# First stage of a hybrid attention block: fixed places for the row sums' transposes, the scaled keys, the query tables, the first gates' weights and the memory's norm

## The chip, the core and the metric

The kernel runs on one core of a Trainium2 chip. A core has five engines with instruction streams of their own: TensorE (PE in the profile; its weight loads are listed as PEld), VectorE (DVE), ScalarE (ACT), GpSimd (POOL) and SyncE (SP), which here issues the DMAs. Matmul results land in PSUM banks and are read from there by DVE and ACT. The metric is the device time of one execution in microseconds (us).

## The reference, cut to what matters

```
h = rms_norm(x, g_pre)                                   # x: 1024 x 1024
a_qkv, bq, bk, bv, mq, ga, gb, gm, mg = split(h @ w_in)
oa = three dilated window attentions of a_qkv, merged by their log-denominators
qb = axial_rope(rms_norm(bq, q_norm)); kb = axial_rope(rms_norm(bk, k_norm))   # 8 and 2 heads of 64
ob = attention(qb, kb, bv)
kvm = rms_norm(mem, g_mem) @ w_mem_kv                    # mem: 256 x 1024
om = attention(mq, km, vm)
y_i = (o_i * silu(gate_i)) @ w_br_i ;  merged = sum sigmoid(mg_i + b_i) * y_i
out = x + rms_norm(merged @ w_out, g_post)
```

The change lies in the first stage alone: the norm of x, the projection of bk and bv, the norm and rotation of the keys, the first two of the twelve silu gate tiles, the norm of the memory.

## The kernel before, in words

Float32 accuracy is had from split operands: a tensor is kept as a rounded high half and a low half (`hh[k]`, `hl[k]` for chunk k of g_pre * x, `wh`, `wl` for weights), and each product takes three matmuls (high x high, low x high, high x low). x is not normalised ahead of the products. Its 1/rms per token is applied to their results instead: as a column per token tile (`rcol`, with `rsq` = rcol squared / 64 and `nrcol` = -rcol), or as a row over all tokens, copied to every partition (`rb`).

**Chunks.** For each of the 8 chunks of x, `x_tile` (L251-256) makes hh and hl, and `x_sq` (L258-263) squares the chunk on ACT and adds it into `acc` on DVE. `kv_proj` (L344-355) is the key and value projection: 8 token tiles T into four PSUM banks, chunk after chunk, 24 matmuls of 128x256 for a chunk. Ahead of chunk 7 it calls `rstd_cols` (L357-363): 8 PE transposes of `acc` (L242), two DVE sums (L243), then the power -1/2 on POOL (L113, L115) for rcol, and rsq and nrcol.

**Keys.** `kv_gen` (L396-415) works on the four banks: `k_norm` (L313-328) squares and rotates a bank's keys with the tables Ck and Sk (DVE) and has POOL make the factor `kss` in four small operations, a power among them (L319-322); `rows_of` (L245-249) spreads rcol by PE transposes into rows, which ACT copies to rb (L405). `kn_mult` (L385-394) multiplies the rotated keys by kss on DVE (L389, tile `kn`) and has ACT scale the values (L394). The query tables Cq and Sq are made on POOL (L449) and are read first by the query projection, at about 102 us.

**Gates.** Two units of the queue: `add_gate` (L196-203) asks for a weight tile of 128x1024 (`load_w`, L95-104: one DMA from SP, high half on ACT L90, low half on DVE L91), runs two halves of 24 matmuls of 128x512 (`dense`, L124-133), each into one of two PSUM banks `d`, and evacuates each half: DVE multiplies by rb (L199), ACT takes the tanh back into the bank (L200), DVE combines the two (L201), and SP stores the result (L202). The bank is free for another half after L201.

**Memory.** `mem_sq` and `mem_prep` (L367-383) make the sum of squares `macc` (ACT, then POOL adds L380, L381, L383) and the halves `mh` (ACT L372) and `ml` (DVE L373) of the memory. Behind the gates come eight units `add_kv` of 24 matmuls of 128x256 (L523), whose weights are prepared by `kv_prep` (L491-498: ACT L496, DVE L497). Unit 0 calls `mem_norm_a` ahead of its first matmul (2 transposes of macc, DVE sum, POOL power, tile `col`) and `mem_norm_b` ahead of the last three (transposes of col back into rows, L248).

**What sets the order.** PE runs in the order written everywhere. `weave` (L161-183) lays the matmuls of the queue's units between the steps of another generator: each step yields a cost, and the generator with the smaller share of its cost done goes next. A matmul of a gate counts 216 of 20736 for the two units, and kv_gen's steps count what it yields of the sum given in the call. Between `manual.__enter__` (L443) and `manual.__exit__` (L473), ACT, DVE and POOL, too, take what is written there in the order written. What is written behind the exit (kn_mult, Cq and Sq, mem_norm_a, kv_prep and all that follows) is placed by the planner, by priority and by its own estimate of when each engine and each operand is free; it may put such instructions between those of the fixed stretch. SP's order is the planner's throughout this stage.

Of the kernel before, what the change touches and what calls it, by code (L numbers as in the profile page):

```python
# [8 lines left out]
F32 = mybir.dt.float32  # L9
R = mybir.dt.float32r  # L10
AF = mybir.ActivationFunctionType
OP = mybir.AluOpType
AX = mybir.AxisListType

D = 1024
S = 1024
NT = 8
P = 128
# [5 lines left out]
B_COS, B_SIN, B_QN, B_QS, B_KN, B_KS = 0, 512, 170, 234, 298, 362  # L24
# [9 lines left out]
def block(ctx: ExitStack, tc: tile.TileContext, x, xT, memT, cst, msk, bcst, tabA, gpost,  # L34
# [77 lines left out]
    def rstd_of(dst, ssq, n, post=None):  # L112
        G.tensor_scalar(dst, ssq, 1.0 / n, EPS, op0=OP.mult, op1=OP.add)  # L113
        w = dst.shape[-1]
        G.tensor_tensor(dst, dst, mhalf[:, :w], op=OP.pow)  # L115
        if post is not None:
            G.tensor_scalar(dst, dst, post, None, op0=OP.mult)
# [22 lines left out]
    def prepare(n):  # L140
        if n == len(queue) and n in early and n not in ready:
            ready[n] = early[n]()
        if n < len(queue) and n not in ready:
            ready[n] = queue[n][0]()
# [16 lines left out]
    def weave(count, att=None, att_cost=0.0, lead=1.0, prio=ATT_PRIO):  # L161
        dg = run_items(count)
        dc = cost_items(count)
        d = a = 0.0
        steps = 0
        live_d, live_a = True, att is not None
        while live_d or live_a:
            if live_d and (not live_a or a / att_cost >= min(1.0, d / dc * lead)):
                try:
                    d += next(dg)  # L170
                    steps += 1
                    if pend and steps % pace[0] == 0:
                        pend.pop(0)()
                except StopIteration:
                    live_d = False
                    d = 1e18
            else:
                try:
                    with tc.high_priority(offset=prio):
                        a += next(att)  # L180
                except StopIteration:
                    live_a = False
# [11 lines left out]
    fp = {}  # L194
# [44 lines left out]
    def cols_of(col, acc, n):  # L239
        p = pst()  # L240
        for T in range(n):
            PE.transpose(p[:, T, :], acc[:, T * 128:T * 128 + 128], ident)  # L242
        V.tensor_reduce(col, p[:, :n], axis=AX.X, op=OP.add)  # L243
# [69 lines left out]
    def k_norm(p, T):  # L313
        n = (slice(None), slice(T, T + 2))
        t1, t2 = kt[0][:, T // 2], kt[1][:, T // 2]
        A.activation(t2, p, AF.Square)
        ss = st.tile([P, 2, 2], F32, name="kss", bufs=4)
        V.tensor_reduce(ss, t2, axis=AX.X, op=OP.add)
        G.tensor_tensor(ss, ss, rsq[n][:, :, None].to_broadcast([P, 2, 2]), op=OP.mult)  # L319
        G.tensor_scalar(ss, ss, EPS, None, op0=OP.add)  # L320
        G.tensor_tensor(ss, ss, mhalf[:, 0:4].rearrange("p (a b) -> p a b", a=2), op=OP.pow)
        G.tensor_tensor(ss, ss, rcol[n][:, :, None].to_broadcast([P, 2, 2]), op=OP.mult)
        V.tensor_tensor(t1, p, tabs["Ck"][n][:, :, None, :].to_broadcast([P, 2, 2, 64]), op=OP.mult)
        for j in range(2):
            a, b = slice(32 * j, 32 * j + 32), slice(32 - 32 * j, 64 - 32 * j)
            V.tensor_tensor(t2[:, :, :, a], p[:, :, :, b], tabs["Sk"][n][:, :, None, a].to_broadcast([P, 2, 2, 32]), op=OP.mult)
        V.tensor_tensor(t1, t1, t2, op=OP.add)
        return t1, ss
# [15 lines left out]
    def kv_proj():  # L344
        banks = [pss1(), pss1(), pss1(), pso()]
        th, tl = wkv
        for k in range(8):
            if k == 7:
                rstd_cols()
            for T in range(NT):  # L350
                dst = banks[T // 2][:, T % 2 * 256:T % 2 * 256 + 256]
                t = slice(T * 128, T * 128 + 128)
                for i, (a, b) in enumerate([(hh[k][:, t], th[:, k]), (hl[k][:, t], th[:, k]), (hh[k][:, t], tl[:, k])]):
                    PE.matmul(dst, a, b, start=k == 0 and T % 2 == 0 and i == 0, stop=k == 7 and T % 2 == 1 and i == 2)
        return banks

    def rstd_cols():  # L357
        for i in range(2):
            cols_of(rcol[:, 4 * i:4 * i + 4], acc[:, i * 512:i * 512 + 512], 4)
        rstd_of(rcol, rcol, D)  # L360
        G.tensor_tensor(rsq, rcol, rcol, op=OP.mult)
        G.tensor_scalar(rsq, rsq, 1.0 / HD, None, op0=OP.mult)
        fp["rstd"] = G.tensor_scalar(nrcol, rcol, -1.0, None, op0=OP.mult)

    mh, mlo, mm, part, kns = [], [], [], [], []

    def mem_prep(c):  # L367
        mh.append(st.tile([P, 4, 256], R, name=f"mh{c}", tag=f"xk{2 + c}"))
        mlo.append(st.tile([P, 4, 256], R, name=f"ml{c}", tag=f"xk{4 + c}"))
        for k in range(4):  # L370
            gcol = cs[:, C_GM + 4 * c + k:C_GM + 4 * c + k + 1]
            A.activation(mh[c][:, k], mt[c][:, k], AF.Copy, scale=gcol)  # L372
            V.scalar_tensor_tensor(mlo[c][:, k], mt[c][:, k], gcol, mh[c][:, k].bitcast(F32), op0=OP.mult, op1=OP.subtract)  # L373
# [11 lines left out]
    def kn_mult(n):  # L385
        t1, ss = part[n]
        kn = st.tile([P, 2, 2, 64], F32, name="kn", bufs=4)
        kns.append(kn)
        V.tensor_tensor(kn, t1, ss[:, :, :, None].to_broadcast([P, 2, 2, 64]), op=OP.mult)  # L389
        for t in range(2):  # L390
            T = 2 * n + t
            vv = banks[n].rearrange("q (t h d) -> q t h d", t=2, h=4)[:, t, 2:4]
            r = rcol[:, T:T + 1]
            A.activation(VS[:, T], vv, AF.Copy, scale=r)  # L394

    def kv_gen(banks):  # L396
        def src(n):
            return banks[n].rearrange("q (t h d) -> q t h d", t=2, h=4)[:, :, 0:2], 2 * n

        for i in range(2):  # L400
            kt.append(st.tile([P, 4, 2, 2, 64], F32, name=f"kt{i}", tag=f"xk{6 + i}"))
        part.extend(k_norm(*src(n)) for n in range(2))
        yield RB_WAIT
        for i in range(2):
            A.activation(rb[:, i * 512:i * 512 + 512], rows_of(rcol[:, 4 * i:4 * i + 4], 4), AF.Copy)  # L405
            yield 436
        for n in range(2, 4):
            part.append(k_norm(*src(n)))
        mem_sq(0)
        yield RB_WAIT + 250  # L410
        mem_prep(0)
        mem_sq(1)
        yield KV_STEP
        mem_prep(1)
        yield KV_STEP


    def b_q(c, w):
# [29 lines left out]
    def table(nm, src, gv, E):  # L448
        E.tensor_tensor(tabs[nm], bt[:, src:src + 512].rearrange("p (t d) -> p t d", t=NT),  # L449
                        cs[:, gv:gv + 64][:, None, :].to_broadcast([P, NT, 64]), op=OP.mult)  # L450
# [5 lines left out]
        if k:  # L456
            x_sq(k - 1)
    x_sq(7)
    table("Ck", B_COS, B_KN, V)
    table("Sk", B_SIN, B_KS, V)  # L460
    banks = kv_proj()
    fp["p"] = st
    add_gate(2, 0)
    add_gate(2, 1)
    prepare(0)
    mt = []
    for c in range(2):
        t = st.tile([P, 4, 256], F32, name=f"mt{c}", tag=f"xk{c}")
        nc.sync.dma_start(t, memT[:, 4 * c:4 * c + 4])
        mt.append(t)  # L470
    weave(2, kv_gen(banks), 872.0 + 2 * RB_WAIT + 2.0 * KV_STEP + KN_PAD, 1.0, 0)
    manual.__exit__(None, None, None)
    for n in range(3, -1, -1):  # L473
        late.append(lambda n=n: kv_out(n, kns[n]))
    for n in range(4):
        kn_mult(n)
    with tc.issue_after(fp["rstd"].ins):
        table("Cq", B_COS, B_QN, G)
        table("Sq", B_SIN, B_QS, G)

    def mem_norm_a():
        mm.append(st.tile([P, 2], F32, name="col"))
        cols_of(mm[2], mm[0], 2)
        with tc.high_priority(offset=200):
            rstd_of(mm[2], mm[2], D)

    def mem_norm_b():
        mm.append(st.tile([P, 256], F32, name="mbc"))
# [24 lines left out]
    def add_kv(u):  # L513
        def gen(w):
            wh, wl = w
            p = psd()
            for k in range(8):
                if u == 0 and k == MN_A:
                    mem_norm_a()
                if u == 0 and k == MN_B:  # L520
                    mem_norm_b()
                for i, (a, b) in enumerate([(wh[:, k, :], mh[k // 4][:, k % 4]), (wh[:, k, :], mlo[k // 4][:, k % 4]), (wl[:, k, :], mh[k // 4][:, k % 4])]):
                    PE.matmul(p[:, 0:256], a, b, start=k == 0 and i == 0, stop=k == 7 and i == 2)  # L523
                    yield 109
                if u and k == KV_K and late:
                    late.pop()()
            kv_evac(u, p)
        queue.append((lambda: kv_prep(u), gen, 24 * 109.0))
# [1685 lines left out]


START_PAD, END_PAD = 700, 300
MN_A, MN_B = 0, 7
KV_K = 5
WR, KV_STEP, RB_WAIT, KN_PAD = 2, 700, 1500, 2800.0
LAG_S, LAG_T, LAG_P, LAG_F = 10, 12, 14, 15  # L2220
BP = 12
B_LEAD, B_PRIO = 1.0, 120
# [121 lines left out]
```

## Time and profile before

| what | us |
|---|---|
| median of three runs | 1389.01 (1386.31, 1389.01, 1389.2) |
| the profiled execution | 1387.79 |
| its span, first to last instruction | 1386.0 |
| PE busy in the span | 1357.5 |
| DVE, ACT, POOL busy | 1013.2, 654.0, 579.3 |

A row of the timeline gives start, duration, engine, line, operation, tile written <- tiles read, shapes and count, and in brackets the idle time of that engine ahead of it with what ended it. Rows of one kind that follow each other are merged: the duration is then that of all of them. Neighbouring operations overlap by some hundredths of a microsecond, so the distance of two starts is a little shorter than the duration.

### The profile page before, as it was taken

The page shows a single profiled execution, that of the slowest core. Times are in us where ns is not written, and L with a number is a line of the kernel's source. Part 1 is how long each engine was busy: PE and PEld are TensorE (multiplying, and loading weights), DVE is VectorE, ACT ScalarE, POOL GpSimd, SP SyncE. Part 2 cuts the span into 40 slices and gives each one's busy share as a digit, 9 for nine tenths or more (in the row PEclk, how much of TensorE's full clock was granted, in tenths as well). Part 3 has the DMA queues.
Part 4 walks back from the last instruction along what each step waited for, and adds up shares of the span by engine and source line. Part 5 has one row for each costly group of instructions (what it writes and reads, how often), then busy time and mean ns, then how long its engine had stood idle before and what let it go on. Part 6 is the DMA issues. An engine that isn't in the chain of part 4 may idle for free.

```text
span 1386.0 us, 22874 instructions
## 1 busy us (share of the span) xinstructions
PE 1357.5 (98%) x8303; PEld 1088.2 (79%) x8303; DVE 1013.2 (73%) x1840; ACT 654.0 (47%) x1384; POOL 579.3 (42%) x443
## 2 busy tenths in 40 slices
PE   7999999999999999999999999999999999989997
PEld 7799987666666789988888888888887777767886
DVE  7768667777777498766777776687786666667977
ACT  6454456656655445323333333333335676653332
POOL 0507702667576200244455455465542143662003
PEclk9999999999999999999999999999999999999999
DMA  6355532322234578514233333332247777886455
GB/s 237 99 188 195 188 117 103 99 74 98 72 125 144 209 233 273 174 54 137 84 121 107 121 107 122 114 106 96 91 128 267 225 220 221 255 229 216 153 185 182
DMA packets 125489, 213.81 MB, mean 154 GB/s; under 512 B 32480, under 2 KB 64576, under 8 KB 125376
## 3 DMA queue, kind: packets, MB, share of 16 engines
q1 hardware_dynamic: 116064, 198.42, 44.5%
q10 hardware_dynamic: 9312, 13.93, 2.8%
q8 instruction: 65, 1.06, 0.3%
q14 instruction: 48, 0.39, 0.1%
HBM read 145.92 MB, written 66.38 MB: 153 GB/s over the span
## 4 chain that ended last, share of the span: by engine, by line
PE 85%; DMA 3%; DVE 3%; POOL 3%; ACT 2%; issue 2%; SPq 1%; DVEq 0%; POOLq 0%; ACTq 0%
PE s L1309 35%; PE d L1885 4%; PE s L1219 4%; PE s L2109 4%; PE ov L804 3%; PE s L1270 3%; PE sc L2027 3%; PE d L128 3%; PE d L130 3%; PE d L132 3%; PE tr L770 2%; PE s L789 2%; PE s L788 2%; PE d L2109 2%; POOL bl L795 1%
## 5 line engine op out<-in xcount | busy, mean ns | idle before, releaser
L795 POOL TENSOR_TENSOR bl<-bl,bp 128x512 f32<-128x512 f32 x96 | 133.1, 1387 | 54.1 <-ACT bp L791 48.6
L1309 PE MATMUL s<-hh,vS 128*128 128x512 f32 x400 | 133.4, 395 | 0.0
L1309 PE MATMUL s<-vA,vS 128*128 128x512 f32 x450 | 106.6, 390 | 0.0
L91 DVE TENSOR_TENSOR vS<-vot,vS 128x512 fp32r<-128x512 f32 x75 | 86.2, 1151 | 19.9 <-ACT vS L90 19.9
L1309 PEld LDWEIGHTS s<-vA,vS 128*128 128x128 f32 x450 | 84.5, 188 | 18.3
L791 ACT ACTIVATE bp<-s 128x512 f32<-128x512 f32 x128 | 75.7, 596 | 43.6 <-PE s L789 42.5
L771 DVE TENSOR_REDUCE bn<-tr 128x1 f32<-128x512 f32 x128 | 85.0, 684 | 13.3 <-PE tr L770 11.9
L128 PE MATMUL d<-hh,wh 128*128 128x512 f32 x224 | 90.0, 402 | 2.4 <-DVE fth L201 2.4
L132 PE MATMUL d<-hh,wl 128*128 128x512 f32 x224 | 90.0, 402 | 0.0
L130 PE MATMUL d<-hl,wh 128*128 128x512 f32 x224 | 89.6, 400 | 0.0
L1309 PEld LDWEIGHTS s<-hh,vS 128*128 128x128 f32 x400 | 75.3, 188 | 17.7
L1309 PE MATMUL s<-hl,vS 128*128 128x512 f32 x200 | 79.1, 395 | 0.0
L1586 ACT ACTIVATE pra<-pra,sts 128x192 f32<-128x192 f32 (+1 forms) x176 | 72.5, 417 | 13.2 <-DVE sts L1585 13.1
L1309 PE MATMUL s<-hh,wh 128*128 128x512 f32 x200 | 78.4, 392 | 0.0
L1309 PE MATMUL s<-hh,wl 128*128 128x512 f32 x200 | 78.4, 392 | 0.0
L1585 DVE CUSTOM_DVE_ANT_0 pra<-s,mask 128x192 f32<-128x192 f32 (+1 forms) x192 | 48.9, 309 | 39.8 <-PE s L1573 31.7
L1309 PE MATMUL s<-hl,wh 128*128 128x512 f32 x200 | 77.8, 389 | 0.0
L1313 ACT ACTIVATE vv<-s 128x512 f32<-128x512 f32 x50 | 30.0, 600 | 85.5 <-PE s L1309 59.0
L1053 POOL TENSOR_TENSOR vot<-wr 128x512 f32<-128x512 f32 x13 | 22.2, 1710 | 112.0 <-DVE vv L1189 112.0
L804 PE MATMUL ov<-bp,VS 128*64 128x512 f32 x256 | 58.5, 598 | 0.0
L1053 POOL TENSOR_TENSOR vot<-vot,vA 128x512 f32<-128x512 f32 x12 | 19.3, 1609 | 90.6 <-DVE vS L91 90.6
L128 PEld LDWEIGHTS d<-hh,wh 128*128 128x128 f32 x224 | 42.5, 190 | 16.3 <-issue 5.5
(627 smaller groups left out, 4009.4 us busy)
## 6 DMA issues: line engine op xcount, KB each, us to landing
wr<-in_wu SPq DMA_DIRECT2D x40, 512.0 KB
vA<-in_wu SPq DMA_DIRECT2D x24, 512.0 KB
qkd<-ko SPq DMA_DIRECT2D x96, 128.0 KB
wl<-thd SPq DMA_DIRECT2D x24, 512.0 KB
wos<-os SPq DMA_DIRECT2D x12, 512.0 KB
wr<-in_wbr SPq DMA_DIRECT2D x24, 256.0 KB
aq<-qkd SPq DMA_DIRECT2D x12, 512.0 KB
ak<-qkd SPq DMA_DIRECT2D x12, 512.0 KB
```

The source lines that it names most:

```text
L91: V.tensor_tensor(dst_l, src, dst_h.bitcast(F32), op=OP.subtract)
L128: PE.matmul(dst, wh[:, k, :], hh[k][:, t], start=k == 0, stop=False)
L130: PE.matmul(dst, wh[:, k, :], hl[k][:, t], start=False, stop=False)
L132: PE.matmul(dst, wl[:, k, :], hh[k][:, t], start=False, stop=k == 7)
L771: fp["last"] = V.tensor_reduce(st[i]["n"][:, j, c:c + 1], s, axis=AX.X, op=OP.min)
L791: A.activation(pp, s, AF.Exp, scale=-1.0)
L795: G.tensor_tensor(lsum[i % 2], lsum[i % 2], pp, op=OP.add)
L804: PE.matmul(o[e * 64:e * 64 + 64], VS[:, kt, kv], d.pop(kt), start=kt < 2, stop=kt >= NT - 2)
L1219: PE.matmul(now[j], a, b, start=k == 0 and q == 0, stop=k == 3 and q == 2)
L1309: PE.matmul(BANK[n, c], a, b, start=k == 0 and q == 0 and not more, stop=k == 3 and q == 2, skip_group_check=c in "XW")
L1586: A.activation(src, src, AF.Exp, scale=-1.0, bias=bias, accum_out=sts[:, 1, h, T:T + 1])
L2109: PE.matmul(dst[:, e[0]:e[1]], a, b, start=k == 0 and q == 0, stop=k == 3 and q == 2)
```

## The change

- `rstd_cols` is called within chunk 7, behind token tiles 0 to 3, and no longer ahead of chunk 7.
- The two gates are queued, and the first one's weights prepared, ahead of `kv_proj`; the tables Ck and Sk stand behind it.
- The first step of kv_gen (k_norm of banks 0 and 1) is taken ahead of the weave, and so ahead of the second gate's weights. The rows of rcol come one matmul later than before (RB_WAIT 1550 in another sum).
- `kn_mult` of banks 0 and 1 stands in front of k_norm of banks 2 and 3, kn_mult of banks 2 and 3 in front of mem_prep of the memory's halves; all four are inside the fixed stretch.
- `mem_norm_a` is the last step of kv_gen, laid between the last matmuls of the gates, with no raised priority.
- Cq and Sq are made on POOL at the end of the fixed stretch, no longer right behind nrcol.

```diff
@@ kv_proj
         for k in range(8):
-            if k == 7:
-                rstd_cols()
             for T in range(NT):
+                if (k, T) == (7, 4):
+                    rstd_cols()
@@ rstd_cols
-        fp["rstd"] = G.tensor_scalar(nrcol, rcol, -1.0, None, op0=OP.mult)
+        G.tensor_scalar(nrcol, rcol, -1.0, None, op0=OP.mult)
@@ kv_gen
         part.extend(k_norm(*src(n)) for n in range(2))
+        yield 0.0
         yield RB_WAIT
         for i in range(2):
             A.activation(rb[:, i * 512:i * 512 + 512], rows_of(rcol[:, 4 * i:4 * i + 4], 4), AF.Copy)
             yield 436
         for n in range(2, 4):
+            kn_mult(n - 2)
             part.append(k_norm(*src(n)))
         mem_sq(0)
-        yield RB_WAIT + 250
+        yield KN_STEP
+        kn_mult(2)
         mem_prep(0)
         mem_sq(1)
         yield KV_STEP
+        kn_mult(3)
         mem_prep(1)
-        yield KV_STEP
+        yield MN_STEP
+        mem_norm_a()
+        yield 0.0
+
+    def mem_norm_a():
+        mm.append(st.tile([P, 2], F32, name="col"))
+        cols_of(mm[2], mm[0], 2)
+        rstd_of(mm[2], mm[2], D)
@@ block, behind the chunks
-    table("Ck", B_COS, B_KN, V)
-    table("Sk", B_SIN, B_KS, V)
-    banks = kv_proj()
     fp["p"] = st
     add_gate(2, 0)
     add_gate(2, 1)
     prepare(0)
+    banks = kv_proj()
+    table("Ck", B_COS, B_KN, V)
+    table("Sk", B_SIN, B_KS, V)
     mt = []
...
-    weave(2, kv_gen(banks), 872.0 + 2 * RB_WAIT + 2.0 * KV_STEP + KN_PAD, 1.0, 0)
+    keys = kv_gen(banks)
+    next(keys)
+    weave(2, keys, RB_WAIT + 872.0 + KN_STEP + KV_STEP + MN_STEP + MN_PAD, 1.0, 0)
+    for nm, src, gv in (("Cq", B_COS, B_QN), ("Sq", B_SIN, B_QS)):
+        table(nm, src, gv, G)
     manual.__exit__(None, None, None)
     for n in range(3, -1, -1):
         late.append(lambda n=n: kv_out(n, kns[n]))
-    for n in range(4):
-        kn_mult(n)
-    with tc.issue_after(fp["rstd"].ins):
-        table("Cq", B_COS, B_QN, G)
-        table("Sq", B_SIN, B_QS, G)
-
-    def mem_norm_a():
-        mm.append(st.tile([P, 2], F32, name="col"))
-        cols_of(mm[2], mm[0], 2)
-        with tc.high_priority(offset=200):
-            rstd_of(mm[2], mm[2], D)
@@ add_kv
-                if u == 0 and k == MN_A:
-                    mem_norm_a()
@@ constants
-MN_A, MN_B = 0, 7
+MN_B = 7
-WR, KV_STEP, RB_WAIT, KN_PAD = 2, 700, 1500, 2800.0
+WR, RB_WAIT, KN_STEP, KV_STEP, MN_STEP, MN_PAD = 2, 1550, 1750, 700, 2700, 500.0
```

## The prediction

> **What bounds the kernel now.** I read the page first, then the waits of PE over the first 140 us, then the timeline of PE, DVE and POOL from 27 to 65 us, and last the windows by stage.
>
> ```profile
> PE 1357.5 (98%) x8303; PEld 1088.2 (79%) x8303; DVE 1013.2 (73%) x1840; ACT 654.0 (47%) x1384; POOL 579.3 (42%) x443
> 300.00:400.00 100.00, 100.00 (x440) 64.49 (x440) 73.45 (x114) 61.62 (x102) 66.02 (x49) 1.00 0.29 95
> ```
>
> PE is busy nearly all the time, and in the middle of the kernel (last row: window, length, busy PE, PEld, DVE, ACT, POOL, granted clock, DMA) without any gap at full clock. So what PE loses in the first stage is paid in full at the end, and what it wins there comes through unless something later takes it. The waits of PE name, after the start, three waits in this stage; the timeline of PE shows where they stand:
>
> ```profile
> 28.48 0.28 PE L354 MATMUL ov<-wbl,hh 128*128 128x256 f32 x1
> 29.90 1.10 PE L242 MATMUL tr<-cs,acc 128*128 128x128 f32 x8 [1.15 <-DVE acc L263]
> ...
> 33.67 0.39 PE L128 MATMUL d<-hh,wh 128*128 128x512 f32 x1
> ...
> 37.78 0.60 PE L248 MATMUL tr<-cs,rcol 128*128 128x128 f32 x4
> ...
> 50.76 0.39 PE L132 MATMUL d<-hh,wl 128*128 128x512 f32 x1
> 53.58 0.50 PE L128 MATMUL d<-hh,wh 128*128 128x512 f32 x1 [2.43 <-DVE fth L201]
> ...
> 60.90 0.36 PE L523 MATMUL d<-mh,wh 128*128 128x256 f32 x1
> ...
> 63.37 0.28 PE L523 MATMUL d<-mh,wl 128*128 128x256 f32 x1
> 64.02 0.43 PE L248 MATMUL tr<-cs,col 128*128 128x128 f32 x2 [0.37 <-POOL col L115]
> ```
>
> The starts give the pace: (37.78 - 33.67) / 18 = 0.23 us for a matmul of 512 columns, (63.37 - 60.90) / 21 = 0.12 for one of 256. By starts, PE loses 29.90 - 28.60 = 1.30 us ahead of the sums' transposes, 53.58 - 50.99 = 2.59 ahead of the fourth gate half, and 64.02 - 63.49 = 0.53 ahead of the memory's rows. A fourth loss is in the windows:
>
> ```profile
> 51.00:55.20 4.20, 1.77 (x8) 1.36 (x8) 4.20 (x5) 3.29 (x7) 2.87 (x3) 0.99 0.27 59
> 55.20:58.60 3.40, 3.40 (x10) 2.66 (x9) 3.40 (x8) 0.00 (x0) 0.79 (x1) 0.51 0.44 158
> ```
>
> Right behind the 2.59 us gap the granted clock stands at 0.51 for 3.40 us: work that at full clock takes 3.40 x 0.51 = 1.73 us, so 1.67 us are lost. Together 1.30 + 2.59 + 1.67 + 0.53 = **6.09 us**.
>
> What stands behind these waits is the order on DVE and POOL:
>
> ```profile
> 27.30 2.55 DVE L263 TENSOR_TENSOR acc<-acc,xk 128x1024 f32<-128x1024 f32 x2
> 29.76 0.69 DVE L449 TENSOR_TENSOR Ck<-bt,cs 128x512 f32<-128x512 f32 x1
> ...
> 30.97 1.28 DVE L243 TENSOR_REDUCE rcol<-tr 128x4 f32<-128x512 f32 x2
> 32.17 2.35 DVE L91 TENSOR_TENSOR wl<-wr,wh 128x1024 fp32r<-128x1024 f32 x2
> 34.43 0.41 DVE L318 TENSOR_REDUCE kss<-kt 128x4 f32<-128x256 f32 x1
> ...
> 35.95 0.41 DVE L318 TENSOR_REDUCE kss<-kt 128x4 f32<-128x256 f32 x1
> ...
> 44.65 0.69 DVE L201 SCALAR_TENSOR_TENSOR fth<-d,fth 128x512 f32<-128x512 f32 x1 [0.67 <-ACT d L200]
> ...
> 48.49 0.69 DVE L199 TENSOR_TENSOR fth<-d,rb 128x512 f32<-128x512 f32 x1
> 49.77 1.49 DVE L389 TENSOR_TENSOR kn<-kt,kss 128x256 f32<-128x256 f32 x1 [0.59 <-POOL kss L322]
> 51.18 1.74 DVE L497 TENSOR_TENSOR wl<-wr,wh 128x1024 fp32r<-128x1024 f32 x1
> 52.85 0.68 DVE L201 SCALAR_TENSOR_TENSOR fth<-d,fth 128x512 f32<-128x512 f32 x1
> 53.45 4.86 DVE L373 SCALAR_TENSOR_TENSOR ml<-mt,cs,mh 128x256 fp32r<-128x256 f32 x8
> ```
>
> The second gate half was multiplied by rb at 48.49, but its bank came free only with L201 at 53.5: the planner had put a kn, which waited for POOL, and the low half of a memory weight between the two. That is the whole gap of the fourth half.
>
> **The change part by part.** *The sums' transposes.* They go behind token tiles 0 to 3 of chunk 7: 12 matmuls x 0.12 = 1.4 us, from 28.60 to 30.0. acc is complete at 27.30 + 2.55 = 29.85, so PE no longer waits, with 0.15 us to spare, and the operands of these 12 matmuls are made ahead of the acc adds in DVE's order, so they are there. Gain 1.30; the first gate begins at about 32.4. If acc were late by more than 0.15, that alone would be lost.
>
> *First gate's weights, Ck and Sk.* DVE makes one low half (2.35 / 2 = 1.18) at 29.76, where two tables took 30.97 - 29.76 = 1.21. So the sums of rcol start at the same 30.97, and the low half is ready about 2 us earlier. The step's DMA keeps its place in SP's queue, as no other DMA is written between the old and the new place. The second gate's weights fall behind two k_norms on DVE, to about 37.6; they are needed by the third half, at 44. Their buffer, and so the second memory weight's load, comes free some 3 us later, and that weight is used behind both gates. Cost: nothing.
>
> *Rows of rcol.* PE stops here if rcol is late. rcol hangs on POOL:
>
> ```profile
> 33.53 2.50 POOL L115 TENSOR_TENSOR rcol<-rcol,mhalf 128x8 f32<-128x8 f32 x1
> ...
> 36.92 1.09 POOL L449 TENSOR_TENSOR Cq<-bt,cs 128x512 f32<-128x512 f32 x1
> ...
> 51.06 0.79 POOL L381 TENSOR_TENSOR macc<-msq 128x256 f32<-128x256 f32 x1
> ```
>
> It is ready at 36.03 in both kernels. PE asks at 37.78 now; 1.30 earlier and one matmul (0.23) later gives 36.7. The margin shrinks from 1.75 to 0.7 and holds: cost nothing, and 0.1 us for each 0.1 that rcol is later than that.
>
> *Cq and Sq leave POOL's queue at 36.92*, so the key factors behind them come 2.1 us sooner, and a kn finds its factor ready. At their new place POOL has only the memory's power ahead of them (queued behind: nothing before the query projection, 40 us later). DVE is busy there, though. Two rows show what that can cost: the kn took 1.49 and the weight's low half 1.74, against 1.18 for each of the pair at 32.17, while POOL worked on its adds (51.06). Bounds: 0, and two tables of 1.09 = 2.2 us on DVE; I take 0 on the path, since the next low half is due only with the next unit.
>
> [...]
>
> *The gates' evacuations* are the core. In the new order L201 stands right behind L199 and waits only for the tanh (0.67 us, row at 44.65), and all of the keys and of the memory keeps its place between the evacuations. The first half ends on PE at about 38.5, the second at 44.0 (32.4 + 48 x 0.23, and some 0.3 for each of the two spreads into rows). From 38.5 DVE has the first evacuation, 0.69 + 0.67 + 0.69 = 2.05, two k_norms of 35.95 - 34.43 = 1.52 and two kn, some 0.4 each where nothing blocks them (an estimate: a k_norm's sum over as many elements takes 0.41): it is through at 44.4. Then L199, tanh, L201: the bank is free at 46.4, needed at 44.0 + 24 x 0.23 = 49.5. **Gain 2.59 + 1.67**, with 3 us to spare, enough for one memory weight (1.74) to slip in again.
>
> What is late next? The third evacuation must free its bank for the first memory unit, at about 55.0. Between the second L199 (44.4) and the third stands what stood there before, from 48.49 to the end of the ml group at 58.3 (9.8 us), plus one more kn (0.4 to 1.49). Of the 9.8, the gap of 0.59 and the blocked parts (1.1 of the kn, 0.56 of the weight, up to about 1.6 of the ml group, if one of its eight takes 0.41) need not recur. So the third L199 begins between 44.4 + 6.4 = 50.8 and 44.4 + 11.2 = 55.6, and its L201 ends 2.0 later: 52.8 to 57.6 against 55.0. Cost between 0 and 2.6; nearest to the rows, with POOL's adds still in the way in part, is 55.6. **I take 0.6.**
>
> *Memory's norm.* macc is there at about 52.2 by the same adds (the second half's square follows the first half's mh on ACT), PE asks at 53.8. The sum on DVE and two POOL steps end at about 57, the rows are wanted at 55.0 + 21 x 0.12 = 57.5: the 0.53 goes. A macc late by more than 1.6 would stop PE in front of the last five gate matmuls.
>
> Sum: 1.30 + 2.59 + 1.67 + 0.53 - 0.6 = **5.5 us** less. The profiled execution took 1387.8, so 1382.3; from the median of the runs, 1389.0, it is 1383.5. I forecast 1383.0.
>
> **The rivals.** *The clock.* [...] As a mechanism of this kernel: the 3.40 slow us come from something else than the gap and stay. Then 5.5 - 1.67 = 3.8 us are won: 1384.7. Chance 0.08.
>
> *The written order isn't kept where it matters*: the planner still lays the memory weight's low half (1.74 us), free to move, ahead of the third L201, or holds it until behind the fixed stretch, where the first memory unit waits for it. About 1.2 to 1.7 us more: 1384.5. Chance 0.12.
>
> *The wait moves.* DVE's fixed list is too long (the upper bound above): the first memory unit waits 2.6 us for its bank, and as after the gap at 50.99 the clock falls, 1.67 more. 6.09 - 4.27 = 1.8 won: 1386.7, no measurable change. For it: DVE has next to no idle time in the list. Against: the tables are out of POOL's way, and kn waits no more. With lesser losses further on: chance 0.15.
>
> *Slower: the planner's later order.* Behind the stage, DVE, ACT and POOL are ordered by the planner's estimate, which changes with the stage. The place to hurt is the attention with POOL's adds, where the chain that ended last leaves PE for POOL:
>
> ```profile
> 285.77 1.28 POOL bl L795
> ```
>
> One more add in front of what PE waits for costs 1.28 us. To end 2.8 us slower, 5.5 + 2.8 = 8.3 us must go, so it decides from seven misplaced adds on: about 1393. For it: the slip at 48.49 shows that one order of the planner cost over 4 us. Against: PE is at 100.00 of 100 us in the window quoted first, so there is slack. Chance 0.10.
>
> **How the numbers follow.** Forecast 1383.0 with chance 0.55; clock 0.08, order 0.12, moved wait 0.15, slower 0.10. About 0.2%, 2.8 us, is what a measurement can tell from no change here. Faster: 0.55 + 0.08 + 0.12 = 0.75; same 0.15; slower 0.10. The range goes from the fastest run less the whole sum (1386.3 - 6.1 = 1380.2) to just beyond the moved wait, 1387.8; outside lie the slower case and a little of the others.
>
> **What would show it.** The sums' transposes at 30.0 without idle; the gates' first matmul at 32.4; no gap between the third and fourth half and clock 1.00 up to 60; the first memory unit at 55 to 56; no wait for col. A wait of PE for L201 ahead of the first memory unit, or clock near 0.5 behind it, is the moved wait; a stop at the rows of rcol says that POOL's power was later than thought; equal times up to 60 us with a longer span mean the later order.

## The result, and the profile after

| | before | after |
|---|---|---|
| median of 18 runs each | 1386.94 us | 1382.93 us |
| lowest to highest | 1384.97 to 1389.84 | 1380.51 to 1385.28 |
| span of the profiled execution | 1386.0 | 1380.9 |

The ratio is 0.9968, with a 95% interval of 0.9961 to 0.9975: 4.4 us less (3.5 to 5.4), or 4.0 by the medians. The two profiled executions differ by 5.1 us.

The page of the changed kernel, its line of PE, and the waits of PE over its first 140 us (total, times, longest):

```profile
PE 1355.4 (98%) x8303; PEld 1086.7 (79%) x8303; DVE 1013.0 (73%) x1840; ACT 653.0 (47%) x1384; POOL 579.8 (42%) x443
```
```profile
PE s L354 <- ACT hh L255: 6.1, 1, 6.1
PE tr L242 <- DVE acc L263: 0.9, 1, 0.9
PE d L525 <- DVE fth L201: 0.6, 1, 0.6
PE s L354 <- DVE hl L256: 0.2, 1, 0.2
```

The work is the same (8303 matmuls). Of the waits in this stage the 2.43 us for L201 and the 0.37 for col are gone. What is left is 0.9 for acc, and a new 0.6 for the third L201. The timeline of PE of the changed kernel places them:

```profile
30.41 1.09 PE L242 MATMUL tr<-cs,acc 128*128 128x128 f32 x8 [0.89 <-DVE acc L263]
...
32.75 0.39 PE L128 MATMUL d<-hh,wh 128*128 128x512 f32 x1
...
37.09 0.60 PE L248 MATMUL tr<-cs,rcol 128*128 128x128 f32 x4
...
50.05 0.39 PE L128 MATMUL d<-hh,wh 128*128 128x512 f32 x1
...
56.48 0.38 PE L525 MATMUL d<-mh,wh 128*128 128x256 f32 x1 [0.57 <-DVE fth L201]
...
59.09 0.38 PE L248 MATMUL tr<-cs,col 128*128 128x128 f32 x2
61.81 0.38 PE L335 MATMUL tr<-cs,kn 128*128 128x128 f32 x2
```

The row at 50.05 is the first matmul of the fourth gate half, without a gap. The window over the last part of the stage, in the changed kernel (the second value is busy PE, the third from the end the granted clock):

```profile
50.00:60.00 10.00, 9.43 (x56) 8.03 (x56) 8.84 (x14) 4.23 (x9) 5.91 (x7) 1.00 0.31 99
```

The granted clock stays at 1.00. The account by stages, from the starts of four kinds of rows and the end of the last acc add (L263), in the two profiled executions:

| stretch | before | after | difference | prediction |
|---|---|---|---|---|
| end of acc to the gates' first matmul | 29.85 to 33.67: 3.82 | 30.35 to 32.75: 2.40 | -1.42 | -1.30 |
| to the first memory matmul (60.90, 56.48) | 27.23 | 23.73 | -3.50 | -2.59 - 1.67 + 0.6 = -3.66 |
| to the transposes of kn (66.80, 61.81) | 5.90 | 5.33 | -0.57 | -0.53 |
| sum | | | -5.49 | -5.5 |

The row of the kernel before with which the third stretch ends:

```profile
66.80 0.38 PE L335 MATMUL tr<-cs,kn 128*128 128x128 f32 x2
```

acc itself came 0.50 later in the execution after (30.35 against 29.85), so the stage ended 4.99 earlier, and the span is 5.1 shorter: nothing was given back behind it (from there to the end it takes 1319.2 us before and 1319.1 after). On DVE of the changed kernel:

```profile
27.81 2.54 DVE L263 TENSOR_TENSOR acc<-acc,xk 128x1024 f32<-128x1024 f32 x2
...
41.05 0.42 DVE L389 TENSOR_TENSOR kn<-kt,kss 128x256 f32<-128x256 f32 x1
...
44.81 0.69 DVE L199 TENSOR_TENSOR fth<-d,rb 128x512 f32<-128x512 f32 x1
45.73 2.24 DVE L501 TENSOR_TENSOR wl<-wr,wh 128x1024 fp32r<-128x1024 f32 x1 [0.23 <-ACT wh L500]
47.89 0.68 DVE L201 SCALAR_TENSOR_TENSOR fth<-d,fth 128x512 f32<-128x512 f32 x1
...
51.45 0.95 DVE L389 TENSOR_TENSOR kn<-kt,kss 128x256 f32<-128x256 f32 x1
52.33 2.14 DVE L373 SCALAR_TENSOR_TENSOR ml<-mt,cs,mh 128x256 fp32r<-128x256 f32 x4
54.39 0.67 DVE L199 TENSOR_TENSOR fth<-d,rb 128x512 f32<-128x512 f32 x1
55.73 0.69 DVE L201 SCALAR_TENSOR_TENSOR fth<-d,fth 128x512 f32<-128x512 f32 x1 [0.67 <-ACT d L200]
```

The planner again laid a memory weight's low half between L199 and L201 of the second half, and it took 2.24 us here. But the two stand 3.7 us earlier than before (44.81 against 48.49), so L201 ends at 48.57, 1.5 us ahead of the matmul at 50.05 that needs its bank. The third L201 ends at 56.42; its bank was wanted at 55.91. The low half does have a share in that wait: the second tanh was done at 46.18, so it held L201 back by 1.7 us, and without it the third L201 would probably have ended ahead of 55.91 (an estimate from these rows).

### The profile page after: what moved, and what is told of

Its sections match the earlier page's. It is cut to its first block, busy times and chain, and to the rows that moved or that the text cites. A ratio compares the mean times of both kernels' runs of the same rounds, so it can differ in the third digit from the quotient of the medians.

```text
span 1380.9 us, 22871 instructions
## 1 busy us (share of the span) xinstructions
PE 1355.4 (98%) x8303; PEld 1086.7 (79%) x8303; DVE 1013.0 (73%) x1840; ACT 653.0 (47%) x1384; POOL 579.8 (42%) x443
## 4 chain that ended last, share of the span: by engine, by line
PE 86%; DVE 4%; DMA 3%; ACT 3%; POOL 2%; issue 2%; SPq 1%; DVEq 0%; POOLq 0%; ACTq 0%
PE s L1311 35%; PE d L1887 5%; PE s L1221 4%; PE s L2111 4%; PE ov L806 3%; PE s L1272 3%; PE sc L2029 3%; PE d L130 3%; PE d L128 3%; PE d L132 3%; PE tr L772 2%; PE s L791 2%; PE s L790 2%; PE d L525 2%; PE d L2111 2%
## 5 line engine op out<-in xcount | busy, mean ns | idle before, releaser
L91 DVE TENSOR_TENSOR vS<-vot,vS 128x512 fp32r<-128x512 f32 x75 | 86.3, 1152 | 19.9 <-ACT vS L90 19.9
L132 PE MATMUL d<-hh,wl 128*128 128x512 f32 x224 | 89.4, 399 | 0.0
```

Of the source, the lines that this page charges most:

```text
L91: V.tensor_tensor(dst_l, src, dst_h.bitcast(F32), op=OP.subtract)
L132: PE.matmul(dst, wl[:, k, :], hh[k][:, t], start=False, stop=k == 7)
```

## The experiments

Each kernel changes one thing in the kernel after, or brings one part of the change to the kernel before. Medians and ratios are against the kernel before, timed alongside (1386.25 us for the first four, 1386.82 for the next four, 1387.47 for the last four). Where an expectation names a theory, it is the prediction's account unless it says otherwise.

**1. Sums' transposes back ahead of chunk 7** (from the kernel after):

```diff
         for k in range(8):
+            if k == 7:
+                rstd_cols()
             for T in range(NT):
-                if (k, T) == (7, 4):
-                    rstd_cols()
```

> The changed kernel, with the sums' transposes back ahead of chunk 7. Theory (PE is set by the end of acc, and all that follows keeps its distance from it): the gates' first matmul comes 3.8 us after the end of acc (2.4 in the changed kernel), all else moves with it, and PE still waits some 0.7 us for the third L201; 1.4 us over the changed kernel, about 1384.3. Rival (from the gates on DVE's list sets the pace, not PE): the third L201 stays where it was, the wait ahead of the first memory unit goes, and only 0.7 us are lost, about 1383.6.

Measured 1383.39, ratio 0.9978 [0.9968, 0.9987]: by the ratios 1.4 us above the 0.9968 of the kernel after, as the theory has it, though the interval reaches from 0 to 2.6, and the median alone lies nearer to the rival's 1383.6. The timeline of PE and two windows of this kernel:

```profile
30.24 1.70 PE L242 MATMUL tr<-cs,acc 128*128 128x128 f32 x8 [1.84 <-DVE acc L263]
```
```profile
27.16:30.57 3.41, 1.57 (x14) 1.36 (x13) 3.31 (x4) 2.00 (x2) 0.00 (x0) 1.00 0.01 4
30.57:33.98 3.41, 3.41 (x18) 3.41 (x17) 3.35 (x6) 0.39 (x1) 1.14 (x2) 0.50 0.44 153
```

The wait is back (1.84), and this time the clock stood at 0.50 for 3.41 us behind it: a gap at the place of the one in the kernel before (1.15) cost 1.7 us more here. From the end of acc (30.18) to the transposes of kn (64.63) it takes 34.45 us, against 31.46 in the kernel after; less 1.71 for the fall, that is 1.28 more, close to the prediction's 1.30. The rest of the stage is that of the kernel after: the wait for the third L201 is 0.6 here too, although PE comes 2.8 us later, so the rival is out, and that wait isn't owed to the earlier start.

**2. The sums' move alone** (on the kernel before, the same edit the other way round).

> The kernel before, with the sums' transposes alone moved behind token tile 3 of chunk 7. Theory: the gates begin 1.4 us earlier, but the bank of the second half still comes free with the late L201 at about 53.5, so the gap ahead of the fourth half grows from 2.6 to about 4 us and the clock still falls: no gain, 1387. Rival (the terms add up): 1.3 us faster, 1385.6.

Measured 1387.47, ratio 1.0004 [0.9994, 1.0015]: nothing won. The waits of PE between 27 and 70 us of this kernel:

```profile
PE d L128 <- DVE fth L201: 2.7, 2, 2.4
PE d L132 <- DVE wl L91: 0.6, 1, 0.6
PE tr L248 <- POOL col L115: 0.4, 1, 0.4
PE tr L242 <- DVE acc L263: 0.2, 1, 0.2
```

PE comes earlier and waits again: 0.6 for the low half of the first gate's weight, which in this kernel still stands behind the tables and the sums, 0.26 for L201 ahead of the third half, and 2.43 ahead of the fourth with the clock fall behind it (54.80 to 58.21; the mean granted clock of this execution is 0.996, against 0.998 in the first one of the kernel after). That last gap is as long as before, and not the 4 us expected, because the move had been spent on the way. The sum is the same: from the end of acc to the transposes of kn it takes 36.94 us (30.25 to 67.19), and 36.95 before. The move gains only together with the evacuations' new order.

**3. The scaled keys alone** (on the kernel before): `kn_mult` at its new places in `kv_gen`, all else as before.

```diff
         for n in range(2, 4):
+            kn_mult(n - 2)
             part.append(k_norm(*src(n)))
...
         yield RB_WAIT + 250
+        kn_mult(2)
         mem_prep(0)
...
         yield KV_STEP
+        kn_mult(3)
         mem_prep(1)
...
-    for n in range(4):
-        kn_mult(n)
```

> The kernel before, with kn_mult alone put into the fixed order, at the places that it has in the changed kernel; sums, tables, weights and the memory's norm as before. Theory: the second L201 comes free of the kn, the gap of 2.6 us and the half clock behind it go, PE waits 0 to 1 us ahead of the first memory unit: 3.3 to 4.3 us faster than before, about 1383. Rival (the tables in POOL's queue hold the key factors up, so kn stops DVE at its new place): less than 2 us faster, over 1385.

Measured 1385.01, ratio 0.9988 [0.9979, 0.9996]: 1.7 us, less than expected, and by the time alone it is the rival's case. In its profile, though, the scaled keys don't stop DVE (the first stands at 42.07, right behind an L201, its factor ready since 41.23), and the stage does win what was expected: no gap ahead of the fourth half, clock 1.00 from 50 to 60 us, a new wait of 0.7 for L201, and the kn transposes at 63.27 instead of 66.80, 3.5 us earlier:

```profile
50.00:60.00 10.00, 9.31 (x52) 7.89 (x51) 9.10 (x15) 5.35 (x10) 4.93 (x6) 1.00 0.24 84
57.59 0.39 PE L524 MATMUL d<-mh,wh 128*128 128x256 f32 x1 [0.69 <-DVE fth L201]
63.27 0.38 PE L335 MATMUL tr<-cs,kn 128*128 128x128 f32 x2
```

Yet its span is only 1.0 shorter than that of before: behind the stage 2.5 us are given back (1321.7 from kn to the end, 1319.2 before). Two windows far behind the stage, in this kernel:

```profile
1196.82:1200.23 3.41, 3.41 (x40) 2.48 (x30) 2.25 (x4) 3.41 (x11) 3.41 (x3) 0.50 0.96 362
1241.19:1244.60 3.41, 3.41 (x9) 2.57 (x10) 1.28 (x2) 3.41 (x5) 1.01 (x2) 0.50 0.52 203
```

Twice the clock fell to 0.50 for 3.41 us, up to 1.7 us each; the profiled execution of before has no fall there (1.00 from 1190 to 1250). The kernel after, run a second time, shows both in its own profile (span 1383.5, at 1195.22 and 1239.59, each 3.41 us at 0.50), so they aren't owed to this edit. The runs' mean granted clocks point the same way: 0.9970 on average over these twelve runs, 0.9981 over the eleven of experiment 4 beside them, which has no fall in the stage either. One fall at half clock takes 1.7 of 1385 us, 0.0012 of the mean, so these runs had about one fall more each, some 1.5 us (an estimate; each run's clock is given to 0.001 only). Why they had more isn't shown.

**4. Query tables earlier on POOL** (from the kernel after): Cq and Sq right behind nrcol, where they stood before.

```diff
         G.tensor_scalar(nrcol, rcol, -1.0, None, op0=OP.mult)
+        for nm, src, gv in (("Cq", B_COS, B_QN), ("Sq", B_SIN, B_QS)):
+            table(nm, src, gv, G)
...
-    for nm, src, gv in (("Cq", B_COS, B_QN), ("Sq", B_SIN, B_QS)):
-        table(nm, src, gv, G)
```

> The changed kernel, with Cq and Sq made on POOL right behind nrcol, in fixed order, as POOL had them before. Theory: the key factors come 2.2 us later, at 41.3 and 43.2, which DVE meets at 41.1 and 42.9: 0.3 to 0.6 us more wait ahead of the first memory unit, 1383.4. Rival (the tables' place is what won): over 2 us slower than the changed kernel, 1385.

Measured 1384.23, ratio 0.9977 [0.9968, 0.9986]: 1.2 us above the kernel after, between the two expectations. DVE and POOL of this kernel meet:

```profile
37.17 1.16 DVE L327 TENSOR_TENSOR kt<-kt,kt 128x256 f32<-128x256 f32 x1
38.25 2.12 DVE L91 TENSOR_TENSOR wl<-wr,wh 128x1024 fp32r<-128x1024 f32 x1
```
```profile
36.96 1.09 POOL L462 TENSOR_TENSOR Cq<-bt,cs 128x512 f32<-128x512 f32 x1
38.01 1.28 POOL L462 TENSOR_TENSOR Sq<-bt,cs 128x512 f32<-128x512 f32 x1
39.25 1.18 POOL L319 TENSOR_TENSOR kss<-kss,rsq 128x4 f32<-128x4 f32 x1
```

The product on DVE took 1.16 (0.42 in the kernel after, at 36.49) and the low half 2.12 (1.22 there), and POOL's product of 4 columns 1.18 (0.20 there). The chain of key factors and memory squares runs later by that and by the tables themselves; PE then waits 0.5 for macc and 1.0 for the third L201, where the kernel after waits 0.57 in all.

**5 and 6. A gap of known length ahead of the first memory unit** (from the kernel after): in the third evacuation (tile 2, second pair, first half), between the tanh and L201, 3 or 5 further products of 512 columns on DVE, whose result nobody reads.

```diff
             A.activation(p, th, AF.Tanh, scale=0.5)
+            if (i, p_, half) == (2, 1, 0):
+                dm = st.tile([P, 512], F32, name="dm")
+                for _ in range(3):          # 5 in the other kernel
+                    V.tensor_tensor(dm, rb[:, 0:512], rb[:, 512:1024], op=OP.mult)
```

> The changed kernel with three products of 128x512 more on DVE between L199 and L201 of the third evacuation (their result is used nowhere), so that PE's wait ahead of the first memory unit grows from 0.7 to about 2.5 us. [...]

> As the gap of three products, with five: PE's wait is about 3.7 us. [...]

With 3, PE waited 1.9 (2.5 expected: one of the products fits into the wait for the tanh). With 5, the timeline of PE of that kernel has

```profile
59.34 0.38 PE L529 MATMUL d<-mh,wh 128*128 128x256 f32 x1 [3.32 <-DVE fth L205]
```

Windows of 3.41 us around these gaps: first those of the kernel with 3 products, then those of that with 5, of which the second is the fall, and the one of the kernel before that ends where its fall begins:

```profile
55.72:59.13 3.41, 1.68 (x14) 1.69 (x15) 3.38 (x6) 1.31 (x2) 1.24 (x3) 1.00 0.21 77
59.13:62.54 3.41, 3.41 (x32) 3.41 (x30) 2.46 (x5) 1.36 (x2) 2.35 (x2) 1.00 0.56 149
```
```profile
57.05:60.47 3.42, 1.13 (x9) 1.13 (x10) 3.35 (x7) 0.22 (x1) 0.68 (x2) 1.00 0.09 35
60.47:63.88 3.41, 3.41 (x18) 3.41 (x18) 1.59 (x3) 0.38 (x1) 2.89 (x3) 0.50 0.53 133
```
```profile
51.70:55.11 3.41, 1.53 (x7) 1.27 (x8) 3.41 (x4) 2.66 (x5) 2.16 (x3) 1.00 0.32 67
```

A 1.9 us gap that left PE busy for 1.68 of 3.41 us cost no clock; the 3.32 us gap, with 1.13 of 3.42, was followed by 3.41 us at 0.50, as were the 1.53 of the kernel before and the 1.57 of experiment 1. In none of these windows was PE idle throughout. By these runs the 1.67 us of the prediction belong to the gap. The single times, one run of each, are 1385.47 and 1390.29 and lie 4.8 apart: of this 1.4 is the longer wait (3.3 - 1.9), 1.7 the fall and 0.4 a later acc (29.89 against 29.45); the last 1.3 come from behind the stage, where the clock of the second kernel fell to 0.50 once more, for 6.83 us from 1200.52 on.

**7. Third evacuation ahead of what stood before it** (from the kernel after): two waits of the fixed order changed, so that the last kn and the second part of the memory come behind the third evacuation.

```diff
-WR, RB_WAIT, KN_STEP, KV_STEP, MN_STEP, MN_PAD = 2, 1550, 1750, 700, 2700, 500.0
+WR, RB_WAIT, KN_STEP, KV_STEP, MN_STEP, MN_PAD = 2, 1550, 1750, 2000, 1400, 500.0
```

> The changed kernel with the second half of the memory (kn of bank 3, mem_prep of half 1) laid behind the third gate evacuation, by KV_STEP 2000 and MN_STEP 1400 in the same sum. Theory (DVE's list ahead of the third L201 is what PE waits for): that wait goes, the first memory unit starts 0.7 us earlier, about 1382.2. Rival (the work is due anyway ahead of the fifth chunk of that unit and PE waits there for ml): no gain, 1382.9.

Measured 1382.67, ratio 0.9966 [0.9955, 0.9977]: as the kernel after. The first memory unit follows without a wait (56.34), but a wait of 0.7 for L201 has taken its place ahead of the second. DVE, then POOL of this kernel:

```profile
57.40 2.18 DVE L501 TENSOR_TENSOR wl<-wr,wh 128x1024 fp32r<-128x1024 f32 x1 [0.17 <-ACT wh L500]
59.51 0.68 DVE L201 SCALAR_TENSOR_TENSOR fth<-d,fth 128x512 f32<-128x512 f32 x1
```
```profile
57.40 1.10 POOL L460 TENSOR_TENSOR Cq<-bt,cs 128x512 f32<-128x512 f32 x1
```

Cq and the low half begin together, and the low half takes 2.18 instead of 1.22.

**8. The same with the sums' transposes two token tiles later**: besides the edit of 7, `(k, T) == (7, 6)` for `(7, 4)`.

> As the kernel with the memory's second half behind the third evacuation, and with the sums' transposes behind token tile 5 instead of 3 of chunk 7. Theory: up to 0.7 us more where PE arrives early at the transposes, nothing where it arrives late, and rcol is still there when PE asks for it (1.7 us to spare now): 1.1 us under the changed kernel, about 1381.8. Rival (rcol comes later and PE stops at the rows): 1383 or more.

Measured 1382.21, ratio 0.9967 [0.9954, 0.9979]. PE has no wait at all between 27 and 70 us. The same two operations met in this kernel, but the low half began a hundredth of a microsecond earlier, and it was POOL's that took longer:

```profile
56.69 1.23 DVE L501 TENSOR_TENSOR wl<-wr,wh 128x1024 fp32r<-128x1024 f32 x1 [0.17 <-ACT wh L500]
```
```profile
56.70 2.17 POOL L460 TENSOR_TENSOR Cq<-bt,cs 128x512 f32<-128x512 f32 x1
```

**9. The memory's norm back behind the fixed stretch** (from the kernel after): ahead of the first memory unit's first matmul, as before.

```diff
         yield MN_STEP
-        mem_norm_a()
-        yield 0.0
...
             for k in range(8):
+                if u == 0 and k == 0:
+                    with tc.high_priority(offset=200):
+                        mem_norm_a()
```

> The changed kernel with the memory's norm (transposes of macc, sum, power) back ahead of the first matmul of the first memory unit, with its raised priority. Theory (PE asks for the rows 2.5 us after that unit begins, and the sum, two POOL steps and a low half of DVE stand in between): the wait for col of about 0.5 us comes back, 0.5 us over the changed kernel, about 1383.4. Rival (other waits cover it): no wait for col, 1382.9.

Measured 1386.13, ratio 0.9993 [0.9984, 1.0002]: 3.5 us above the kernel after, where half a microsecond was expected. With the memory's power gone from the fixed order, POOL reaches the tables at 52.94, and they meet the ml group. DVE, then POOL, then the wait of PE in this kernel:

```profile
52.31 3.82 DVE L373 SCALAR_TENSOR_TENSOR ml<-mt,cs,mh 128x256 fp32r<-128x256 f32 x4
```
```profile
52.94 1.28 POOL L458 TENSOR_TENSOR Cq<-bt,cs 128x512 f32<-128x512 f32 x1
54.18 1.27 POOL L458 TENSOR_TENSOR Sq<-bt,cs 128x512 f32<-128x512 f32 x1
```
```profile
PE d L526 <- DVE fth L201: 2.3, 1, 2.3
```

The four ml took 3.82 instead of 2.14, the third L201 came 1.7 later (57.40 against 55.73), PE waited 2.3, and the clock fell to 0.50 behind it (59.46 to 62.87). The wait for col that was expected didn't come back: in this execution the rows, at 61.77, come late enough. So the norm's new place is worth more than the 0.53 us of its own wait: in POOL's queue it also keeps the tables off DVE's list. This is the prediction's rival of the moved wait, and it needed only one collision.

**10. First gate's weights late again** (from the kernel after): Ck and Sk ahead of the projection, `prepare(0)` behind it.

```diff
-    prepare(0)
-    banks = kv_proj()
     table("Ck", B_COS, B_KN, V)
     table("Sk", B_SIN, B_KS, V)
+    banks = kv_proj()
+    prepare(0)
```

> The changed kernel with Ck and Sk back ahead of kv_proj and the first gate's weights behind it, so that on DVE the tables come before rcol's sums and the low half after them. Theory: the low half is late for the first gate's third matmul, where PE arrives early (0.6 us of wait in the run with the sums alone), and POOL's first step for rcol runs beside the low half and takes 1.10 instead of 0.57 us, the power 2.50 instead of 1.96; rcol about 1 us later, still ahead of PE: up to 0.6 us over the changed kernel, about 1383.4. Rival (the order of these three on DVE makes no difference): POOL's steps as in the changed kernel, no wait for wl, 1382.9.

Measured 1384.09, ratio 0.9973 [0.9962, 0.9984]: 0.7 above the kernel after, inside both intervals. Its profile shows the price: PE waits 0.6 for the first gate's low half (L132 for L91). By this row that part of the change is worth about half a microsecond, once the sums have moved; the times alone don't tell it from nothing. The delay of rcol that was expected hardly came: it is there 5.34 us after acc, against 5.04 in the kernel after.

**11 and 12. The kernel after and kernel 8 once more, side by side.**

> The changed kernel once more, beside the kernel with the third evacuation first and later sums, on one chip. Theory: its gain depends on when the clock first rises in an execution, through where PE stands at the last chunk; 1382.9, 4 us under before. Rival: the same stage times in every execution.

> The kernel with the memory's second half behind the third evacuation and the sums' transposes behind token tile 5, once more, beside the changed kernel. Theory: no wait of PE between the sums and the second memory unit, 0.5 to 1.0 us under the changed kernel, about 1382.2. Rival: no difference, 1382.9.

1382.6, ratio 0.9968 [0.9959, 0.9978], and 1381.5, ratio 0.9965 [0.9953, 0.9977]: no difference that can be told. In this execution of the kernel after, PE came to chunk 7 1.1 us ahead of acc and didn't wait for it; in the first one it was 2.4 us ahead. That varies with the start: the clock first rises at 9.6 to 13.2 us in the 14 executions profiled here (in the kernel before the matmuls of 256 columns start 0.21 us apart up to 10.64 and 0.12 apart from 10.81 on), and the later it does, the smaller is PE's lead over acc (2.4 us at 9.62, none at 13.19 and 13.23; correlation -0.91). In this execution of kernel 8 the low half (56.80) began 20 ns behind Cq (56.78) and took 2.19, Cq 1.12, and PE waited 0.7; in the first one, where it began 10 ns ahead, the low half took 1.23 and Cq 2.17.

## Why the prediction was right

The time came out at 1382.93, within the range. That it lies only 0.07 from the forecast is luck: the forecast was 6.0 us below the median of three runs, 1389.01, but over 18 runs the kernel before took 1386.94, and 4.4 us were won (3.5 to 5.4), less than the sum of 5.5. A base 2.1 us too high and a gain too large cancelled. The mechanism is borne out by the profiles, where the stage won 5.49 us counted from acc:

- *The gates' evacuations, 2.59 + 1.67*: right. Gap and fall are gone, and experiment 3 has both gone by the scaled keys alone. That the fall belonged to the gap, against the clock rival, is shown by experiments 1, 5 and 6. Whether every execution pays it isn't shown: both executions profiled with this gap (before and experiment 2) had the fall, while behind the wait of 1.9 us in experiment 5 there was none. If some executions have none, that would take part of the difference between 5.5 and 4.4; no run here tells how many.
- *The new wait, 0.6 of a possible 0 to 2.6*: 0.57, 0.6 or 0.7 in four further executions, and 1.0 in experiment 4. It is no fixed quantity, though: with one more collision (experiment 9) it was 2.3. From the second to the third L199 DVE took 9.58 us (44.81 to 54.39), between the 6.4 and 11.2 of the bounds; that the value chosen between them was the right one is luck.
- *col, 0.53*: gone. The rows came 1.6 us later than foreseen (59.09 for 57.5), col 0.8 (57.83 for 57): the margin was larger than thought.
- *The sums' transposes, 1.30*: the mis-sized term. The step said that 12 matmuls of cover leave acc 0.15 us to spare. In the profiled execution after, PE still waited 0.89. What varies is when PE reaches chunk 7 against acc. From the starts and waits of the 14 executions profiled here, PE would have waited 0 to 2.3 us there without the move; the move saves the smaller of that and 1.4, on average 0.9 us (an estimate from these rows). Experiment 1 puts it at 1.4 by the times, give or take 1.6 from the two intervals, and at 1.28 in its profile without the fall, in an execution where PE was early; experiment 2 shows that without the other parts it is worth nothing.
- *rcol's power unchanged at 36.03*: wrong, and harmless. POOL of the changed kernel:

```profile
32.77 0.57 POOL L113 TENSOR_SCALAR rcol<-rcol 128x8 f32<-128x8 f32 x1 [32.34 <-DVE rcol L243]
33.43 1.96 POOL L115 TENSOR_TENSOR rcol<-rcol,mhalf 128x8 f32<-128x8 f32 x1
```

  rcol is there at 35.39, although acc came 0.5 later. Counted from the end of acc, rcol takes 5.04 us here and took 6.18 before, where two low halves of DVE stood at this place. L113 takes 0.57 here beside the tables, 1.10 in the kernel before and in experiment 10 beside a low half; in the latter rcol takes 5.34. So the margin at the rows is 1.7 us (37.09 - 35.39) instead of the feared 0.7.
- *The rival of the written order*: its condition came true (the low half at 45.73), its price didn't come on top, since the second evacuation now has the room that the step had counted for it, and the delay of the third is within the 0.6.
- *Slower by a later order*: not seen; the gain of the stage is that of the span, 4.99 and 5.1.

Left open: how the 4.4 us divide exactly. Experiment 3's median has only 1.7 of the 3.5 us that its profile shows in the stage; by the estimate given there its lower clocks account for most of the rest; why they were lower isn't shown. The single parts don't add up (1.7 for the keys, nothing for the sums alone, but 1.4 lost where they are taken out).

## What to carry to other kernels

An engine's evacuation chain that frees a bank belongs together in its queue; what slips in between costs a gap on PE as soon as it takes longer than the bank has room, and here up to 1.7 us more in clock behind waits of 1.84, 2.3, 2.43 and 3.32 us, though none behind one of 1.9. Moving one operation earlier is worth only what isn't waited for at the next place, so parts that gain nothing alone (experiment 2) can be worth having with the others, and a part that looks small (experiment 9) may hold something else in its place. Where operations of two engines meet and one of them takes longer for it, as DVE's low half (2.18 us in experiment 7, 1.22 in the kernel after) or POOL's Cq (2.17 in experiment 8, 1.10 in experiment 7) did here, look at who starts first, to some hundredths of a microsecond.

## What the runs showed of the hardware

**The clock.** The falls measured between the start and the last stretch of the kernel go to 0.50 and last 3.41 us (before: 55.11 to 58.52; experiment 1: 30.57 to 33.98), one of them twice that (6.83, from 1200.52 with 5 products). They don't start at the same place in every execution: 1196.82 and 1241.19 in experiment 3, 1195.22 and 1239.59 in the second one of the kernel after, 44.37 apart in both.

The length of the wait alone doesn't sort the cases of the first stage. A fall came behind 1.84 us (experiment 1), 2.3 (experiment 9), 2.43 (before) and 3.32 (5 products); none behind 1.15 (before, ahead of the sums' transposes) and 1.9 (3 products).

Nor does PE's share of 3.41 us alone. In the window that ends where a fall begins PE was busy for 0.33 of it (5 products, at 60.47), 0.39 (experiment 9), 0.45 (before), 0.46 (experiment 1, and with 5 products at 1200.52), 0.50 and 0.52 (experiment 3), 0.53 (experiment 7, at 1238.58) and 0.55 (experiment 8, at 1237.10). No fall followed the windows with 0.49 (3 products, 55.72 to 59.13), 0.50 (experiment 8, 1192.73 to 1196.14), 0.56 (5 products, 1241.48 to 1244.89) and 0.66 (before, 27.81 to 31.22). The second half of the double fall came behind a window at 0.50 in which PE was busy for 0.62. What decides isn't shown by these runs.

**The later falls.** At about 1195 to 1244 us the clock falls to 0.50 in some of the profiled executions (experiment 3, the second one of the kernel after) and not in others (before, the first one of the kernel after: 1.00 from 1190 to 1250), for up to 1.7 us each. From the kn transposes to the end, the five profiled executions (of several kernels) without such a fall took 1317.5 to 1320.9 us, the six with one 1318.5 to 1321.5, the three with two (or a double one) 1321.7 to 1322.3. Over 71 runs of the kernel before, a longer time goes with a lower mean clock (correlation -0.64). So the falls are a likely reason for part of the 5 us between the fastest and the slowest run of one kernel; the overlap of the ranges says that they aren't the only one.

**DVE and POOL.** In the cases named here, in which operations of the two ran side by side, one of them took longer than elsewhere. A small one did, too: L113 on col, 128x2, took 1.09 beside a low half (experiment 9, at 59.10) and 0.19 in the kernel after. In experiments 8 and 12 the one that started first kept its time (the low half 1.23, Cq 1.12) and the other took longer (Cq 2.17, the low half 2.19); in 7 both rows read 57.40, Cq took 1.10 and the low half 2.18. It was seen with a scalar_tensor_tensor as well: the four ml took 3.82 beside Cq and Sq (experiment 9) and 2.14 in the kernel after.
